# The block sums of two down projections, on VectorE between its low parts instead of on GpSimd in one run

## The chip, the cores and the metric

The kernel runs on one core of a Trainium2 chip. Its engines work side by side, each through its own queue in order: TensorE multiplies matrices, VectorE and ScalarE work element by element, GpSimd does so more slowly, and SyncE issues the DMAs. They wait for each other on semaphores. The metric is the device time of one launch in microseconds (us), the median of three runs.

## What is computed

Two layers of a transformer-like trunk on an input of 1024 tokens by 1024 channels, all in float32. Each layer has a mixer (a gated MLP over chunks in the first, differential attention in the second) and then a convolutional feed-forward part; both stand between RMS norms. The change touches only the last product of the feed-forward part:

```python
def conv_ffn(x, w_up, conv_w, conv_b, w_down):
    h = causal_dwconv(x @ w_up, conv_w, conv_b)
    g, u = h[..., :D_FF], h[..., D_FF:]
    return (jax.nn.gelu(g) * u) @ w_down

# in each of the two layers, after the mixer
y = rmsnorm(h, norm_g[layer, 2])
y = conv_ffn(y, ffn_w_up[layer], ffn_conv_w[layer], ffn_conv_b[layer], ffn_w_down[layer])
h = h + rmsnorm(y, norm_g[layer, 3])
```

Here `x @ w_up` is 1024x1024 by 1024x5632, and the product with `w_down`, the down projection, is 1024x2816 by 2816x1024. It is done twice, once for each layer.

## The kernel before

Float32 matmuls are made of three matmuls in a reduced format. `split` (L167 to L173) takes a tile apart into a high part (a cast on ScalarE, L170) and a low part (the tile minus its high part, on VectorE, L173), and TensorE adds up high x high, high x low and low x high (L162, `PASSES`).

`down` (L459) makes a down projection by a Strassen-Winograd scheme with seven products in place of eight. The activations are cut into four blocks A11, A12, A21, A22 of 512 tokens by 1408 channels, the weights likewise. Sums of weight blocks (T1 to T4) were made earlier, while the feed-forward part ran, and lie in the buffer `td` in HBM. The sums of activation blocks are made here, in place, by `combine` (L482): A21 becomes A21 + A22, then A11 becomes A21 - A11, then A22 becomes A22 - A11 and A12 becomes A12 - A11. The products run in the order A11·B11, A22·T4, A12·B21, A11·T2, A21·T1, A12·B22, A22·T3 (L528 to L552); the first three use blocks as they were loaded, the last four their sums. So a sum may overwrite a block only once its old content has been split, and must be there before the product that uses it.

A block is eleven tiles of 128 channels by 512 tokens, handled in five pairs of two tiles (128x1024 elements) and one piece of one tile (128x512). One block sum is thus five instructions of 128x1024 and one of 128x512, and a down projection has four block sums, 24 instructions, all issued by `nc.gpsimd.tensor_tensor` in L484. `product` (L498) splits activations and weights pair by pair (`operands`, L486) and multiplies: 11 tiles x 4 groups of rows x 3 passes make 132 matmuls of 128x512 for one product. The last two pieces of a product (its tail) are multiplied group by group, so that the four results come out one after another.

How far the splits run ahead of TensorE is set by the buffers: 15 tiles `t8` for activation blocks and their parts, 7 tiles `w4` for the parts of weights, 4 tiles `wr` for weights as they are loaded. A buffer is taken again when its last reader is done. All loads stand in one queue, SyncE's, and a load that waits for a buffer holds up the loads behind it. The order in which instructions stand on each engine is set by a scheduler when the program is built, from the order of the code, the dependences and its own estimate of times; it may move an instruction ahead of others that stand before it in the code.

In the profile the activation tiles are all called t, loaded weights wr, their parts w, matmul results ps.

Of the kernel before, what the change touches and what calls it, by code (L numbers as in the profile page):

```python
# [13 lines left out]
ALU = mybir.AluOpType  # L14
# [46 lines left out]
SHORT_TAIL = 2  # L61
# [3 lines left out]
def trunk(ctx: ExitStack, tc: tile.TileContext, io):  # L65
    nc = tc.nc
# [7 lines left out]
    def nm(s):  # L74
        uid[0] += 1
        return f"{s}_{uid[0]}"

    def t8(dt=F32R, shape=(P, 2, S)):
        return base.tile(list(shape), dt, tag="t8", name=nm("t8"), bufs=15)
# [88 lines left out]
    def split(hi, lo, src, engine=None, pin=False):  # L168

        i = nc.scalar.copy(hi, src)  # L170
        if pin:
            tc.keep_in_program_order(i)
        return (engine or nc.vector).tensor_tensor(lo, src, hi.bitcast(F32), ALU.subtract)  # L173

    def raw_w(src, a, b):
        raw = wpool.tile([P, a, b], F32, tag="wr", name=nm("wr"), bufs=4)
        nc.sync.dma_start(raw, src)
        return raw

    def w4(shape, extra=None):  # L180

        pool, tag, n = extra or (wpool, "w4", 7)
        return pool.tile([P] + list(shape), F32R, tag=tag, name=nm(tag), bufs=n)
# [263 lines left out]
    def weight_blocks(w, o):  # L447
        nk = o.shape[1]
        return {
            "B11": lambda k, n: w[k:k + n, :, 0:512],  # L450
            "B21": lambda k, n: w[nk + k:nk + k + n, :, 0:512],
            "B22": lambda k, n: w[nk + k:nk + k + n, :, 512:1024],
            "T1": lambda k, n: o[0, k:k + n, :, 0],
            "T3": lambda k, n: o[0, k:k + n, :, 1],
            "T4": lambda k, n: o[1, k:k + n, :, 0],
            "T2": lambda k, n: o[1, k:k + n, :, 1],
        }

    def down(l, h_in, h_out, g_post, g_pre, y_next):  # L459

        nk = NFF // 2
        pairs = [(k, min(2, nk - k)) for k in range(0, nk, 2)]
        weights = weight_blocks(io["ffn_down"][l], td[l])
        raw = {}

        def load(a):  # L470
            half, j = int(a[1]) - 1, (int(a[2]) - 1) * nk
            raw[a] = []
            for k in range(0, nk, 4):
                n = min(4, nk - k)
                t = t8(F32, (P, 4, 512))
                nc.sync.dma_start(t[:, :n], pd[l][half, j + k:j + k + n].rearrange("j p c -> p j c"))
                raw[a].append(t)

        def of(a, k, n):
            return raw[a][k // 4][:, k % 4:k % 4 + n]  # L480

        def combine(o, a, b, op):  # L482
            for k, n in pairs:
                nc.gpsimd.tensor_tensor(of(o, k, n), of(a, k, n), of(b, k, n), op)  # L484

        def operands(a, b, k, n, apart=False):  # L486
            x = t8(F32R, (P, 2, 2, 512))
            split(x[:, 0, :n], x[:, 1, :n], of(a, k, n))
            raw = raw_w(weights[b](k, n).rearrange("k p c -> p k c"), n, 512)
            if apart:  # L490
                t = t8(F32R, (P, 2, 2, 512))
                w = t[:, 0, :n], t[:, 1, :n]
            else:
                w = w4((n, 512)), w4((n, 512))
            split(*w, raw)
            return x, w

        def product(a, b, ahead=(), first=None, at=3, tail=SHORT_TAIL, wide=0):  # L498

            out = [bank1() for _ in range(4)]  # L500

            def part(i, k, n, x, w):
                for kt in range(k, k + n):
                    for m, (p, q) in enumerate(PASSES):
                        mm(
                            out[i], x[:, q, kt - k, i * P:(i + 1) * P], w[p][:, kt - k, :],
                            kt == 0 and m == 0, kt == nk - 1 and m == 2,
                        )

            for m, (k, n) in enumerate(pairs[:-tail]):  # L510
                xw = ahead[m] if m < len(ahead) else operands(a, b, k, n)
                for i in range(4):
                    part(i, k, n, *xw)
                if m == at and first:
                    first()
            xws = [operands(a, b, k, n, m >= tail - wide) for m, (k, n) in enumerate(pairs[-tail:])]
            for i in range(4):
                for (k, n), xw in zip(pairs[-tail:], xws):
                    part(i, k, n, *xw)
                yield i, out[i]  # L520

        add = nc.vector.tensor_tensor
        load("A11")
        ahead = [operands("A11", "B11", *pairs[0])]
        yield
        with tc.tile_pool(name=nm("out"), bufs=1) as pool:
            u2, c11, v = (pool.tile([P, 4, 512], F32, tag=n, name=nm(n)) for n in ("u2", "c11", "v"))
            for i, r in product("A11", "B11", ahead, lambda: load("A22")):  # L528
                nc.scalar.copy(u2[:, i], r)
            gp = load_g(pool, g_post)  # L530
            gn = load_g(pool, g_pre) if g_pre is not None else None
            load("A21")
            for i, r in product("A22", "T4", (), lambda: load("A12"), 1):
                nc.scalar.copy(v[:, i], r)

            combine("A21", "A21", "A22", ALU.add)
            combine("A11", "A21", "A11", ALU.subtract)
            combine("A22", "A22", "A11", ALU.subtract)
            for i, r in product("A12", "B21"):
                add(c11[:, i], r, u2[:, i], ALU.add)  # L540
            combine("A12", "A12", "A11", ALU.subtract)
            for i, r in product("A11", "T2"):
                add(u2[:, i], r, u2[:, i], ALU.add)
                nc.gpsimd.tensor_tensor(v[:, i], v[:, i], u2[:, i], ALU.add)
            u4 = t8(F32, (P, 4, 512))
            for i, r in product("A21", "T1"):
                add(u4[:, i], r, u2[:, i], ALU.add)
            for i, r in product("A12", "B22"):
                c12 = pool.tile([P, 512], F32, tag="c12", name=nm("c12"), bufs=2)
                add(c12, r, u4[:, i], ALU.add)  # L550
                end(pool, i, (c11[:, i], c12), h_in, h_out, gp, gn, y_next, n=2)
            for i, r in product("A22", "T3", tail=TAIL, wide=WIDE):  # L552
                add(v[:, i], r, v[:, i], ALU.add)
                add(u4[:, i], r, u4[:, i], ALU.add)
                end(pool, 4 + i, (v[:, i], u4[:, i]), h_in, h_out, gp, gn, y_next, n=2)
# [483 lines left out]
    class Winograd:  # L1039
# [32 lines left out]
        def add(self, o, a, b):  # L1072
            nc.vector.tensor_tensor(o, a, b, ALU.add)  # L1073
# [251 lines left out]
```

## Time and profile before

| | us |
|---|---|
| median of 3 runs | 2198.74 (2196.4 to 2199.98) |
| the profiled execution, its time | 2199.97 |
| its span, first to last instruction | 2198.2 |
| TensorE busy | 2127.0 (97%) |
| VectorE busy | 1696.9 (77%) |
| ScalarE busy | 1095.6 (50%) |
| GpSimd busy | 895.4 (41%) |

The profile is of one execution. Its time is 1.23 us above the median of the runs. The busy share is an average over the whole program: a TensorE that is busy 97% of the time can still lose time in the places where it waits, and where its clock falls after a wait. The two down projections lie from about 747 to 945 us and from about 1967 to 2190 us after the first instruction. A busy VectorE or GpSimd instruction may be a slow one: the profile counts the time from its start to its end, whatever held it up inside.

### The profile page before, as it was taken

What the parts mean: (1) busy time and instruction counts of PE and PEld (TensorE: products, weight loads), DVE (VectorE), ACT (ScalarE), POOL (GpSimd) and SP (SyncE); (2) the same over time, 40 slices, a digit from 0 to 9 for tenths busy, and PEclk for the clock granted to TensorE, in tenths of its full rate; (3) what the DMA queues carried; (4) which work ended last, traced back from release to release, by engine and by line L of the source; (5) the groups of instructions that cost most, each with busy time, mean ns of one, the idle gap of its engine ahead of it and who ended that gap; (6) DMA issues with size and microseconds to landing.
All of it is one profiled execution on the core that took longest, in us unless ns stands there. A gap on an engine that the chain in (4) does not pass through costs nothing.

```text
span 2198.2 us, 27299 instructions
## 1 busy us (share of the span) xinstructions
PE 2127.0 (97%) x10008; PEld 1730.1 (79%) x10008; DVE 1696.9 (77%) x1983; ACT 1095.6 (50%) x1923; POOL 895.4 (41%) x739
## 2 busy tenths in 40 slices
PE   8989998999999999999999999999899999999998
PEld 6868776888888877887777777778688888887786
DVE  5755569888888798688588888866987888878856
ACT  7423445555545544464366665655554555553433
POOL 1463135666666094042001001322565667618512
PEclk9989999999999999999999999999999999999999
DMA  8332422444444652353411110243244444456224
GB/s 316 101 125 77 179 82 98 170 163 157 141 155 161 225 191 92 130 182 105 156 44 44 55 43 20 87 144 116 77 149 140 163 154 153 163 191 230 87 96 167
DMA packets 159270, 292.82 MB, mean 133 GB/s; under 512 B 12704, under 2 KB 77088, under 8 KB 159136
## 3 DMA queue, kind: packets, MB, share of 16 engines
q1 hardware_dynamic: 159136, 291.08, 38.4%
q8 instruction: 78, 1.28, 0.2%
q14 instruction: 56, 0.46, 0.1%
HBM read 214.49 MB, written 76.55 MB: 132 GB/s over the span
## 4 chain that ended last, share of the span: by engine, by line
PE 74%; DVE 9%; ACT 3%; issue 1%; DMA 1%; POOL 0%; DVEq 0%; POOLq 0%; ACTq 0%; SPq 0%
PE ps L162 69%; PE pst L162 2%; DVE t L173 2%; DVE w L173 2%; PE pst L887 1%; ACT e L868 1%; DVE t L1138 1%; PE pst L334 1%; DVE cols L1073 1%; DVE xs L344 0%; DVE e L874 0%; DVE h L381 0%; DMA wr<-td 0%; DVE sm L865 0%; ACT t L1136 0%
## 5 line engine op out<-in xcount | busy, mean ns | idle before, releaser
L162 PE MATMUL ps<-t,w 128*128 128x512 f32 x4848 | 1152.8, 394 | 20.4 <-ACT tm L1069 7.8
L162 PEld LDWEIGHTS ps<-t,w 128*128 128x128 f32 x4848 | 901.1, 189 | 221.6 <-issue 12.3
L162 PE MATMUL ps<-w,t 128*128 128x512 f32 x2512 | 600.5, 396 | 23.6 <-DVE t L173 13.6
L162 PEld LDWEIGHTS ps<-w,t 128*128 128x128 f32 x2512 | 474.7, 191 | 126.4 <-DVE t L173 16.1
L173 DVE TENSOR_TENSOR w<-wr,w 128x512 fp32r<-128x512 f32 (+1 forms) x274 | 333.3, 1224 | 165.1 <-ACT w L170 84.1
L170 ACT CAST w<-wr 128x512 fp32r<-128x512 f32 (+1 forms) x276 | 219.1, 802 | 206.3 <-PE ps L162 196.7
L1138 DVE SCALAR_TENSOR_TENSOR t<-cols,cw,t 128x1023 f32<-128x1023 f32 (+1 forms) x176 | 265.0, 1506 | 18.6 <-ACT t L1136 16.7
L484 POOL TENSOR_TENSOR t<-t,t 128x1024 f32<-128x1024 f32 (+1 forms) x48 | 146.8, 3096 | 116.7 <-PE ps L162 58.4
L173 DVE TENSOR_TENSOR t<-t,t 128x1024 fp32r<-128x1024 f32 (+1 forms) x124 | 179.3, 1477 | 16.6 <-ACT t L170 16.5
L173 DVE TENSOR_TENSOR w<-wt,w 128x512 fp32r<-128x512 f32 x176 | 171.4, 984 | 14.4 <-ACT w L170 14.3
L1069 ACT COPY tm<-ps 128x512 f32<-128x512 f32 x136 | 79.1, 582 | 146.8 <-PE ps L162 146.7
L1027 POOL TENSOR_TENSOR wt<-wr,wr 128x512 f32<-128x512 f32 x44 | 68.0, 1544 | 195.6 <-DMA wr<-in_ffn_up 140.2
L170 ACT CAST t<-t 128x1024 fp32r<-128x1024 f32 (+1 forms) x124 | 105.7, 888 | 74.0 <-PE ps L162 50.4
L1136 ACT ACTIVATE t<-cols,cw 128x1024 f32<-128x1024 f32 x88 | 109.7, 1247 | 60.3 <-DVE cols L1073 60.2
L162 PE MATMUL ps<-t,t 64*128 64x512 f32 (+4 forms) x792 | 129.2, 375 | 0.8 <-ACT e L868 0.4
L376 POOL TENSOR_SCALAR sm<-sm 128x1 f32<-128x1 f32 x32 | 22.3, 698 | 245.6 <-ACT y L374 245.3
L202 POOL TENSOR_SCALAR sm<-sm 128x1 f32<-128x1 f32 (+1 forms) x42 | 12.8, 305 | 264.7 <-ACT ot L907 161.3
L170 ACT CAST w<-wt 128x512 fp32r<-128x512 f32 x176 | 108.0, 622 | 22.7 <-PE ps L162 13.6
L162 PEld LDWEIGHTS ps<-t,t 64*128 64x128 f32 (+1 forms) x792 | 91.1, 187 | 34.5 <-issue 11.2
L868 ACT ACTIVATE e<-ps,sm 128x128 f32<-128x128 f32 (+7 forms) x128 | 94.3, 745 | 28.8 <-DVE sm L860 22.8
L173 POOL TENSOR_TENSOR t<-wr,t 128x1024 fp32r<-128x1024 f32 (+1 forms) x16 | 36.4, 2282 | 168.8 <-ACT t L170 168.8
L1073 DVE TENSOR_TENSOR cols<-ps,tm 128x512 f32<-128x512 f32 x132 | 90.1, 682 | 17.1 <-PE ps L162 15.4
(156 smaller groups left out, 2443.8 us busy)
## 6 DMA issues: line engine op xcount, KB each, us to landing
wr<-in_ffn_up SPq DMA_DIRECT2D x88, 512.0 KB, 4.2
wr<-in_ffn_down SPq DMA_DIRECT2D x94, 256.0 KB, 3.8
pd<-t SPq DMA_DIRECT2D x88, 256.0 KB, 2.6
td<-wr SPq DMA_DIRECT2D x88, 256.0 KB, 2.5
wr<-td SPq DMA_DIRECT2D x40, 512.0 KB, 3.7
t<-pd SPq DMA_DIRECT2D x16, 1024.0 KB, 8.2
wr<-in_ffn_down SPq DMA_DIRECT2D x30, 512.0 KB, 3.6
hd<-h SPq DMA_DIRECT2D x24, 512.0 KB, 2.6
```

The source lines that it names most:

```text
L162: nc.tensor.matmul(o, a, b, start=first, stop=last, skip_group_check=onto)
L170: i = nc.scalar.copy(hi, src)
L173: return (engine or nc.vector).tensor_tensor(lo, src, hi.bitcast(F32), ALU.subtract)
L334: nc.tensor.transpose(pt[:, k * P:(k + 1) * P], xs[:, f:f + P], ident)
L376: nc.gpsimd.tensor_scalar(ss, sq[:, 0:1], sq[:, 1:2], EPS, ALU.add, ALU.add)
L484: nc.gpsimd.tensor_tensor(of(o, k, n), of(a, k, n), of(b, k, n), op)
L868: nc.scalar.activation(e[:, :L], si[i], AF.Exp, bias=negm[:, i:i + 1], accum_out=sm[:, i:i + 1])
L1027: i = nc.gpsimd.tensor_tensor(t1, b12, b11, ALU.subtract)
L1069: nc.scalar.copy(t, o)
L1073: nc.vector.tensor_tensor(o, a, b, ALU.add)
L1136: nc.scalar.activation(tt, src, AF.Identity, bias=c[:, 3:4], scale=c[:, 2:3])
L1138: nc.vector.scalar_tensor_tensor(tt[:, tap:], src[:, :S - tap], c[:, 2 - tap:3 - tap], tt[:, tap:], ALU.mult, ALU.add)
```

## The change

`combine` no longer issues anything. It appends its six instructions to a list, and a new function `some(n)` issues the next n of them, on VectorE. `product` calls `some(2)` after it has split a pair (in the product A22·T4 only from the third pair on, since A21 is being loaded then) and once more at the tail. The calls of `combine` for A21 and A11 move ahead of the product A22·T4, and those for A12 and A22 stand behind A12·B21; calls of `some(len(sums))` issue what is left. The function bodies that are left out here are the same as before.

```diff
@@ -479,9 +479,16 @@
+        sums = []
+
         def combine(o, a, b, op):
+
             for k, n in pairs:
-                nc.gpsimd.tensor_tensor(of(o, k, n), of(a, k, n), of(b, k, n), op)
+                sums.append((of(o, k, n), of(a, k, n), of(b, k, n), op))
+
+        def some(n):
+            for _ in range(min(n, len(sums))):
+                nc.vector.tensor_tensor(*sums.pop(0))
...
             for m, (k, n) in enumerate(pairs[:-tail]):
                 xw = ahead[m] if m < len(ahead) else operands(a, b, k, n)
+                if m > 1 or b != "T4":
+                    some(2)
                 for i in range(4):
                     part(i, k, n, *xw)
...
+            some(4 if tail == SHORT_TAIL else len(sums))
             for i in range(4):
...
             load("A21")
+
+            combine("A21", "A21", "A22", ALU.add)
+            combine("A11", "A21", "A11", ALU.subtract)
             for i, r in product("A22", "T4", (), lambda: load("A12"), 1):
                 nc.scalar.copy(v[:, i], r)
-
-            combine("A21", "A21", "A22", ALU.add)
-            combine("A11", "A21", "A11", ALU.subtract)
-            combine("A22", "A22", "A11", ALU.subtract)
             for i, r in product("A12", "B21"):
                 add(c11[:, i], r, u2[:, i], ALU.add)
+            some(len(sums))
             combine("A12", "A12", "A11", ALU.subtract)
+            combine("A22", "A22", "A11", ALU.subtract)
             for i, r in product("A11", "T2"):
                 add(u2[:, i], r, u2[:, i], ALU.add)
                 nc.gpsimd.tensor_tensor(v[:, i], v[:, i], u2[:, i], ALU.add)
+            some(6 - (12 - len(sums)))
...
             for i, r in product("A21", "T1"):
                 add(u4[:, i], r, u2[:, i], ALU.add)
+            some(len(sums))
```

The scheduler decides where the sums then stand. VectorE's queue in the first down projection, before the change, at the splits of the second product A22·T4. L173 are low parts; a row names the result, the two inputs and the shape. t_975, t_979, t_986, t_990 are low parts of pairs 0 to 3 of A22, w_978, w_982, w_989, w_993 those of T4's pairs 0 to 3:

```order
L173 TENSOR_TENSOR w_978_6236<-wr_6233,w_977_6235 128x1024
L173 TENSOR_TENSOR t_975_6230<-t_955_6152,t_975_6230 128x1024
L173 TENSOR_TENSOR t_979_6263<-t_955_6152,t_979_6263 128x1024
L173 TENSOR_TENSOR w_982_6269<-wr_6266,w_981_6268 128x1024
L173 TENSOR_TENSOR t_986_6302<-t_956_6154,t_986_6302 128x1024
L173 TENSOR_TENSOR t_990_6335<-t_956_6154,t_990_6335 128x1024
L173 TENSOR_TENSOR w_989_6308<-wr_6305,w_988_6307 128x1024
L173 TENSOR_TENSOR w_993_6341<-wr_6338,w_992_6340 128x1024
```

Nothing else stands between the low parts. After the change, the same place of VectorE's queue up to the low part of T4's pair 1 (L491 are the sums; t_968 to t_970 hold A21, t_955 to t_957 A22, t_923 to t_925 A11, four tiles or three in each):

```order
L173 TENSOR_TENSOR w_978_6236<-wr_6233,w_977_6235 128x1024
L491 TENSOR_TENSOR t_968_6220<-t_968_6220,t_955_6152 128x1024 x2
L173 TENSOR_TENSOR t_975_6230<-t_955_6152,t_975_6230 128x1024
L491 TENSOR_TENSOR t_969_6222<-t_969_6222,t_956_6154 128x1024
L173 TENSOR_TENSOR t_979_6263<-t_955_6152,t_979_6263 128x1024
L491 TENSOR_TENSOR t_969_6222<-t_969_6222,t_956_6154 128x1024
L173 TENSOR_TENSOR w_982_6269<-wr_6266,w_981_6268 128x1024
```

Four sums now stand among the first low parts, two of them ahead of the first low part of A22. The rows that follow these after the change, up to T4's pair 3:

```order
L491 TENSOR_TENSOR t_970_6224<-t_970_6224,t_957_6156 128x1024
L491 TENSOR_TENSOR t_970_6224<-t_970_6224,t_957_6156 128x512
L491 TENSOR_TENSOR t_923_5922<-t_968_6220,t_923_5922 128x1024 x2
L173 TENSOR_TENSOR t_986_6302<-t_956_6154,t_986_6302 128x1024
L491 TENSOR_TENSOR t_924_5924<-t_969_6222,t_924_5924 128x1024
L173 TENSOR_TENSOR t_990_6337<-t_956_6154,t_990_6337 128x1024
L491 TENSOR_TENSOR t_924_5924<-t_969_6222,t_924_5924 128x1024
L491 TENSOR_TENSOR t_925_5926<-t_970_6224,t_925_5926 128x1024
L173 TENSOR_TENSOR w_989_6308<-wr_6305,w_988_6307 128x1024
L173 TENSOR_TENSOR w_993_6343<-wr_6340,w_992_6342 128x1024
```

Seven more sums stand ahead of the low part w_989. From the first sum to w_989 the queue has 16 instructions of 128x1024 and one of 128x512, of which the last is w_989 itself. In the second down projection VectorE's queue has as many, 16 and one, from its first sum to the low part of T4's pair 2; there one sum, not two, stands ahead of T4's pair 0. The remaining sums follow in both among the splits of A22·T4's tail and behind them, and the last seven, A22's last piece and A12's six, between the splits of A12·B21, so that all are queued ahead of the adding up of A12·B21's results.

TensorE's queue changes at one place, the start of pair 2 of A22·T4 in the first down projection. Before (ps_971 and ps_972 are the results of the first two groups of rows, w_988 and w_989 the high and low part of the weights):

```order
L162 MATMUL ps_971_6226<-w_988_6307,t_986_6302 128x512 x2
L162 MATMUL ps_971_6226<-w_989_6308,t_986_6302 128x512
L162 MATMUL ps_971_6226<-w_988_6307,t_986_6302 128x512 x2
L162 MATMUL ps_971_6226<-w_989_6308,t_986_6302 128x512
L162 MATMUL ps_972_6227<-w_988_6307,t_986_6302 128x512 x2
```

and after:

```order
L162 MATMUL ps_971_6226<-w_988_6307,t_986_6302 128x512 x2
L162 MATMUL ps_972_6227<-w_988_6307,t_986_6302 128x512 x2
L162 MATMUL ps_971_6226<-w_989_6308,t_986_6302 128x512
L162 MATMUL ps_971_6226<-w_988_6307,t_986_6302 128x512 x2
L162 MATMUL ps_971_6226<-w_989_6308,t_986_6302 128x512
```

The first matmul that needs the low part w_989 stands two matmuls later. GpSimd's queue loses its 48 sums; ScalarE's queue is the same, and SyncE's differs in two loads that change places.

## Rows read from the trace of the kernel before

**Rows 1.** The page's first part: busy us (share) x instructions of each engine.

```profile
PE 2127.0 (97%) x10008; PEld 1730.1 (79%) x10008; DVE 1696.9 (77%) x1983; ACT 1095.6 (50%) x1923; POOL 895.4 (41%) x739
```

**Rows 2.** Chain that ended last, first down projection: start us, us, what.

```profile
775.86 7.63 DMA wr<-td
...
784.60 3.34 DVE w L173
...
799.65 2.78 DVE t L173
...
836.46 2.75 DVE t L173
```

**Rows 3.** Timeline of TensorE, first down: start, us, instructions, [idle before <-releaser].

```profile
746.93 40.51 PE L162 MATMUL ps<-w,t 128*128 128x512 f32 x178
787.99 12.33 PE L162 MATMUL ps<-w,t 128*128 128x512 f32 x53 [0.55 <-DVE w L173]
802.48 30.48 PE L162 MATMUL ps<-w,t 128*128 128x512 f32 x126 [2.16 <-DVE t L173]
833.72 1.66 PE L162 MATMUL ps<-w,t 128*128 128x512 f32 x6 [0.76 <-DVE t L173]
839.26 104.43 PE L162 MATMUL ps<-w,t 128*128 128x512 f32 x449 [3.88 <-DVE t L173]
943.53 6.28 PE L162 MATMUL ps<-t,t 128*128 128x512 f32 x27
```

**Rows 4.** Timeline of TensorE, second down projection.

```profile
1967.51 40.51 PE L162 MATMUL ps<-w,t 128*128 128x512 f32 x178
2009.72 12.35 PE L162 MATMUL ps<-w,t 128*128 128x512 f32 x53 [1.71 <-DVE w L173]
2024.19 30.46 PE L162 MATMUL ps<-w,t 128*128 128x512 f32 x126 [2.12 <-DVE t L173]
2055.42 1.65 PE L162 MATMUL ps<-w,t 128*128 128x512 f32 x6 [0.76 <-DVE t L173]
2060.96 104.54 PE L162 MATMUL ps<-w,t 128*128 128x512 f32 x449 [3.88 <-DVE t L173]
2165.33 24.64 PE L162 MATMUL ps<-t,t 128*128 128x512 f32 x108
```

**Rows 5.** Stretches: us, busy us (x) PE, PEld, DVE, ACT, POOL; PEclk, DMA share, GB/s.

```profile
770.00:844.00 74.00, 66.65 (x273) 53.55 (x273) 69.34 (x25) 26.79 (x32) 73.58 (x24) 0.93 0.47 161
1989.00:2063.00 74.00, 65.52 (x274) 52.69 (x274) 70.55 (x26) 28.14 (x34) 73.09 (x24) 0.95 0.48 167
```

**Rows 6.** Timeline of GpSimd: the sums of both down projections.

```profile
770.06 73.58 POOL L484 TENSOR_TENSOR t<-t,t 128x1024 f32<-128x1024 f32 x24 [58.37 <-PE ps L162]
...
1989.29 71.07 POOL L484 TENSOR_TENSOR t<-t,t 128x1024 f32<-128x1024 f32 x23 [57.68 <-DMA t<-pd]
```

**Rows 7.** Timeline of VectorE, first down: as the sums begin and after their end.

```profile
767.81 1.22 DVE L173 TENSOR_TENSOR w<-wr,w 128x1024 fp32r<-128x1024 f32 x1 [4.80 <-PE ps L162]
770.02 1.23 DVE L173 TENSOR_TENSOR t<-t,t 128x1024 fp32r<-128x1024 f32 x1 [0.98 <-ACT t L170]
771.59 2.99 DVE L173 TENSOR_TENSOR t<-t,t 128x1024 fp32r<-128x1024 f32 x1 [0.34 <-ACT t L170]
...
853.41 1.22 DVE L173 TENSOR_TENSOR w<-wr,w 128x1024 fp32r<-128x1024 f32 x1
854.55 1.22 DVE L173 TENSOR_TENSOR t<-t,t 128x1024 fp32r<-128x1024 f32 x1
...
932.10 0.68 DVE L173 TENSOR_TENSOR t<-t,t 128x512 fp32r<-128x512 f32 x1
932.70 0.68 DVE L550 TENSOR_TENSOR c<-ps,t 128x512 f32<-128x512 f32 x1
```

**Rows 8.** A float32 tensor_tensor on VectorE, L1143: ns min/median/max, first and last start.

```profile
L1143 DVE TENSOR_TENSOR t<-t,t x44: 1210/1218/2325, 362.3 to 1973.7; 128x1024 f32<-128x1024 f32 x44
```

**Rows 9.** ScalarE's cast of T4's pair 2, first down: what it waited for.

```profile
783.51 1.05 ACT L170 CAST w<-wr 128x1024 fp32r<-128x1024 f32 x1 [0.88 <-DMA wr<-td]
```

## The prediction

> **What bounds the kernel now.** First the page's busy times: TensorE is busy 97% [rows 1], so time is lost only where it waits or is slowed. Then the chain of waits in the first down projection: it leaves TensorE in three places, all between 775 and 839 us, and each time comes back to it through low parts on VectorE [rows 2]. TensorE's timeline gives the waits: 0.55, 2.16, 0.76 and 3.88 us, 7.35 together, each ended by a low part [rows 3]. In the second down projection there are four again, 8.47 together [rows 4].
>
> What the two projections lose in all is read from the same rows. From 746.93 to 943.53 us, 196.60 us, TensorE has 178 + 53 + 126 + 6 + 449 = 812 matmuls [rows 3]. The first 178 run without a wait at 40.51 / 178 = 0.2276 us each, so 812 would take 184.8 us: 11.8 us are lost. From 1967.51 to 2165.33, 197.82 us, as many matmuls lose 13.0 us [rows 4]. Together **24.8 us**. Not all of it is waiting: in the 74 us around the sums the granted clock is 0.93 and 0.95 [rows 5], so part of the time ran at 1.2 in place of 2.4 GHz, which costs 74 x (0.07 + 0.05) = 8.9 us. The clock fell after TensorE had waited, so this part goes if the waits go.
>
> Why the low parts are late: GpSimd's sums run from 770.06 to 843.6 and from 1989.29 on [rows 6], and in just that time VectorE's low parts are slow. One of 128x1024 takes 1.22 us at 767.81 and at 853.41, but 2.99 at 771.59 [rows 7] and 3.34 at 784.60 [rows 2]. VectorE is busy 69.34 and 70.55 of the 74 us with 25 and 26 instructions [rows 5], so its low parts come at the rate at which it can make them, and TensorE overtakes it.
>
> **The change part by part.** *The sums leave GpSimd.* They had the 73.58 us beside the low parts [rows 6]; GpSimd's other work there is none. A low part should go back to its own price: back to back, starts are 854.55 - 853.41 = 1.14 us apart for 128x1024 and 932.70 - 932.10 = 0.60 for 128x512 [rows 7].
>
> *The sums join VectorE.* A float32 tensor_tensor of the same shape and kinds as a sum takes 1.218 us in the median [rows 8], as long as a low part alone, so a sum is taken at 1.14 and 0.60 too: 20 x 1.14 + 4 x 0.60 = 25.2 us for each projection. With 25 low parts at 1.14 or less (28.5) VectorE then has at most 53.7 us of work in a stretch that lasts some 62 us once nothing is lost (74 - 11.8), so it no longer is the slowest there. The bounds of a sum's price: 1.14 from the rows of the same shape, and 1.22 plus a little if each waits for the end of the one before.
>
> *What is queued behind the sums.* VectorE works in order, so what matters is the low parts behind sums. The first sum of each projection needs A21 to be loaded; GpSimd's first sum began at 770.06 and 1989.29 [rows 6], so VectorE's is taken to begin then (in the second, its low part at 1988.4 moves behind this sum, which costs nothing while TensorE is still in the product before). The critical one is the low part of T4's pair 2: 16 instructions of 128x1024 and one of 128x512 from the first sum to its end make 16 x 1.14 + 0.60 = 18.8 us. It is done at 788.9 and 2008.1. Its weights are no limit: their cast started at 783.51 [rows 9], behind loads that the change doesn't touch. TensorE came to this low part at 787.99 - 0.55 = 787.4 and at 2009.72 - 1.71 = 2008.0 [rows 3, 4]; in the first projection its queue now has two other matmuls before it, 2 x 0.23, which makes it 787.9. So it will wait 788.9 - 787.9 = 1.0 and 0.1 us, where it waited 0.55 and 1.71. The low parts before it have more room: pair 0's, behind two sums, is done some 3.4 us after the first sum, 773.5, and the product begins at 787.4 less 50 matmuls, 776.0.
>
> *After that* the queue empties faster than TensorE asks. Behind w_989 follow, up to the last low part of A22·T4's tail, four instructions of 128x1024 (one of them a sum) and three of 128x512 (one a sum): 4 x 1.14 + 3 x 0.60 = 6.4 us, so 795.3; before, TensorE stood still for it from 800.3 on [rows 3]. The second projection has six and three there, 8.6 us, 2016.7 against a need at about 2020. Among A12·B21's splits stand the last seven sums: ten low parts and five sums of 128x1024, two and two of 128x512, 19.5 us in the 30 us of a product. The waits of 2.16, 0.76 and 3.88 us should go, and the fallen clock with them: after the wait of 1.71 us at 2009.72 the next 53 matmuls still took 12.35 / 53 = 0.233 us each [rows 4], so a wait of 1.0 us is taken to leave the clock alone.
>
> *The rest* has no cost on the path. The two loads that change places on SyncE, and GpSimd's queue, which only gets shorter, wait for nothing that is late. From 839 us on TensorE ran 449 matmuls without a wait [rows 3], with sums of A22 and A12 long done; these products find the same order of VectorE's queue as before.
>
> **The sum.** 24.8 lost - 1.1 for the new waits = 23.7 us. From the profiled execution's own 2199.97 us this gives 2176.3; the median of the runs is 1.23 lower, so 2175.0 against 2198.74.
>
> **The rivals.** *Sums that come out slower (A).* If VectorE's instructions don't overlap at all, each is 0.1 us longer, 16 of them 1.6: the waits at pair 2 become 2.6 and 1.7 us. Waits of about 2.16 us were the ones behind which the clock fell; the first such stretch has 126 matmuls in 30.48 us [rows 3], 1.8 us over 126 x 0.2276. With one such fall in each projection 2.6 + 1.7 + 2 x 1.8 = 7.9 of the 24.8 stay lost, 16.9 are gained: 2182. For it: eleven of the sums do stand ahead of that one low part. Against it: starts 1.14 apart in [rows 7].
>
> *A wait that comes back at A11·T2 (B).* The largest wait before, 3.88 us, came there. If the sums of A12 and A22 between A12·B21's splits keep VectorE behind, it stays, with 0.76 ahead of it and the fallen clock behind it, 104.43 - 449 x 0.2276 = 2.2 us: 2 x 6.8 = 13.7 of the 24.8, and 1.1 at pair 2. Gained are 10.0: 2189. Against it: 19.5 us of work in 30.
>
> *VectorE becomes the bound (C), the slower side.* If the low parts are slow for a reason of their own, not for GpSimd's sums, VectorE keeps its 69.34 and 70.55 us [rows 5] and gets 25.2 on top: 94.5 and 95.8 in a stretch of 74, so TensorE waits 20.5 and 21.8 us more: 2198.7 + 42 = 2241. It decides from the point where a low part beside no GpSimd work still takes more than about 1.9 us ((74 - 25.2) / 25). For it, a little: the low part that began at 770.02, with the first sum, still took 1.23 us. Against it: all before that and from the last sum's end on are fast too [rows 6, 7]. The Trainium skill has a rule by which this rival would be the forecast: its page Perfetto Trace Analysis, section Identifying the Most-Contended Engine, says to read for VectorE and GpSimd the engine with the highest occupancy as the bottleneck, and 94% busy is VectorE's here; by that rule, adding work to it makes the kernel slower, about 2241 as just worked out. The trace speaks against taking the occupancy at its word, since most of a busy time of 2.99 us is not work.
>
> **How the numbers follow.** The forecast has 0.72, A 0.13, B 0.06, C 0.05; 0.04 are left for gains that vanish elsewhere, so that the time stays within 0.2%, about what a measurement of this kernel can tell from no change. Faster are the forecast, A and B: 0.91. Slower is C: 0.05. Same: 0.04. The range goes from all 24.8 us gained and a median 2.5 lower, as the runs spread, 2171.5, to beyond A, 2186; it leaves out B, C and the rest.
>
> **What would show it.** In the changed kernel's profile no sum is on GpSimd; low parts and sums of 128x1024 on VectorE take 1.22 us in both down projections; TensorE has one wait of about 1 us at the third pair of A22·T4 of the first projection and nearly none else in them; the granted clock there is 1.00; and 812 matmuls take 186 us from the start of A11·B11. Low parts over 2 us would make C right, a wait of 3 us at A11·T2 B, a fallen clock after pair 2 A. Waits of TensorE outside the two projections that are not in the kernel before would make the sum wrong.

## The result and the profile after

The changed kernel takes **2173.69 us** in the median (2172.96 to 2175.61), the kernel before, on the same chip, 2197.57: a ratio of 0.9892, with a 95% interval of 0.988 to 0.9904. The prediction was 2175.0, in a range of 2171.5 to 2186.

The profiled execution took 2173.85 us, its span is 2172.0. Busy times first, as in [rows 1]:

```profile
PE 2115.5 (97%) x10008; PEld 1722.7 (79%) x10008; DVE 1662.3 (77%) x2031; ACT 1094.9 (50%) x1923; POOL 748.5 (34%) x691
```

VectorE has 48 instructions more, the sums, and yet is busy 34.6 us less than in [rows 1]. So its sums were paid for by shorter low parts. Both are seen in the trace. All sums by their line (ns min/median/max, first and last start), and VectorE's timeline in the first down projection (start, us, instruction, [idle before <-releaser]), which answers to [rows 7]:

```profile
L491 DVE TENSOR_TENSOR t<-t,t x48: 677/1214/1227, 771.7 to 2032.0; 128x1024 f32<-128x1024 f32 x40, 128x512 f32<-128x512 f32 x8
```

```profile
769.09 1.23 DVE L173 TENSOR_TENSOR w<-wr,w 128x1024 fp32r<-128x1024 f32 x1 [4.80 <-PE ps L162]
771.72 2.36 DVE L491 TENSOR_TENSOR t<-t,t 128x1024 f32<-128x1024 f32 x2 [1.40 <-DMA t<-pd]
774.00 1.22 DVE L173 TENSOR_TENSOR t<-t,t 128x1024 fp32r<-128x1024 f32 x1
775.14 1.21 DVE L491 TENSOR_TENSOR t<-t,t 128x1024 f32<-128x1024 f32 x1
...
787.09 2.35 DVE L491 TENSOR_TENSOR t<-t,t 128x1024 f32<-128x1024 f32 x2
789.36 2.35 DVE L173 TENSOR_TENSOR w<-wr,w 128x1024 fp32r<-128x1024 f32 x2
```

No sum takes over 1.227 us, and the low parts between them take 1.22, where [rows 7] had 2.99. Starts are 1.14 us apart: 774.00, 775.14.

What TensorE makes of it, in the first and then the second down projection, against [rows 3, 4]:

```profile
748.21 40.96 PE L162 MATMUL ps<-w,t 128*128 128x512 f32 x180
790.63 143.55 PE L162 MATMUL ps<-w,t 128*128 128x512 f32 x632 [1.46 <-DVE w L173]
934.02 6.29 PE L162 MATMUL ps<-t,t 128*128 128x512 f32 x27
...
1955.12 184.22 PE L162 MATMUL ps<-w,t 128*128 128x512 f32 x812
2139.17 24.64 PE L162 MATMUL ps<-t,t 128*128 128x512 f32 x108
```

Of four waits in each projection one is left in all, 1.46 us. The 812 matmuls take 185.81 us in place of 196.60, and 184.05 (1955.12 to 2139.17) in place of 197.82: 10.79 and 13.77 us less, **24.56** together. The stretches of the first projection (us, busy us (x) of PE, PEld, DVE, ACT, POOL; PEclk, DMA share, GB/s) answer to [rows 5]:

```profile
746.90:931.50 184.60, 183.14 (x808) 151.38 (x807) 131.26 (x130) 86.12 (x106) 11.73 (x11) 1.00 0.48 165
770.00:832.00 62.00, 60.54 (x267) 49.83 (x266) 51.69 (x50) 27.20 (x34) 0.00 (x0) 1.00 0.58 202
```

The granted clock is 1.00 where it was 0.93, and around the sums VectorE does 50 instructions in 51.69 us where it did 25 in 69.34.

The spans differ by 2198.2 - 2172.0 = 26.2 us. The two projections give 24.56. The first begins 1.28 us later than before, the time between them is 2.88 us shorter (1021.10 from 934.02 to 1955.12; it was 1023.98), and the end is 0.04 us shorter. Between the projections the code is the same; in the executions of the experiments below this time is 1019.8 (without sums) to 1024.7 us (sums fixed in place). So the 2.88 us are taken as scatter from one execution to the next.

### The profile page after: what moved, and what is told of

Read it like the earlier page. It is cut to its first block, busy times and chain, and to the rows that moved or that the text cites. A ratio compares the mean times of both kernels' runs of the same rounds, so it can differ in the third digit from the quotient of the medians.

```text
span 2172.0 us, 27266 instructions
## 1 busy us (share of the span) xinstructions
PE 2115.5 (97%) x10008; PEld 1722.7 (79%) x10008; DVE 1662.3 (77%) x2031; ACT 1094.9 (50%) x1923; POOL 748.5 (34%) x691
## 3 DMA queue, kind: packets, MB, share of 16 engines
q8 instruction: 78, 1.28, 0.2%
## 4 chain that ended last, share of the span: by engine, by line
PE 69%; DVE 9%; ACT 4%; DMA 3%; issue 2%; POOL 2%; SPq 0%; DVEq 0%; POOLq 0%; ACTq 0%
PE ps L162 65%; PE pst L162 2%; DVE t L173 2%; DVE w L173 1%; DVE t L1151 1%; ACT e L881 1%; PE pst L900 1%; PE pst L334 1%; DMA wr<-in_ffn_up 1%; DVE cols L1086 1%; DMA t<-pd 1%; DVE e L887 0%; DVE xs L344 0%; DMA td<-wr 0%; DVE sm L878 0%
## 5 line engine op out<-in xcount | busy, mean ns | idle before, releaser
L162 PE MATMUL ps<-w,t 128*128 128x512 f32 x2512 | 590.2, 392 | 10.5 <-ACT w L170 6.1
L162 PEld LDWEIGHTS ps<-w,t 128*128 128x128 f32 x2512 | 469.4, 188 | 108.3 <-ACT w L170 6.3
L173 DVE TENSOR_TENSOR w<-wr,w 128x512 fp32r<-128x512 f32 (+1 forms) x274 | 292.1, 1072 | 168.7 <-ACT w L170 77.5
L173 DVE TENSOR_TENSOR w<-wt,w 128x512 fp32r<-128x512 f32 x176 | 171.4, 984 | 16.4 <-ACT w L170 16.2
L173 DVE TENSOR_TENSOR t<-t,t 128x1024 fp32r<-128x1024 f32 (+1 forms) x124 | 133.9, 1108 | 14.4 <-ACT t L170 14.0
L555 POOL TENSOR_TENSOR v<-v,u 128x512 f32<-128x512 f32 x8 | 12.0, 1498 | 306.8 <-DVE u L554 306.8
L173 POOL TENSOR_TENSOR t<-wr,t 128x1024 fp32r<-128x1024 f32 (+1 forms) x16 | 36.4, 2286 | 166.3 <-ACT t L170 158.1
```

Of the source, the lines that this page charges most:

```text
L162: nc.tensor.matmul(o, a, b, start=first, stop=last, skip_group_check=onto)
```

## The experiments

All ratios are against the kernel before, run on the same chip. "Wait" is TensorE's in the first down projection, and "low part" the duration of one of 128x1024 there up to 860 us (behind that GpSimd adds up v, and a low part beside these additions takes up to 2.32 us even where GpSimd has no sums).

| kernel | median us | ratio (95%) | wait us | low part us |
|---|---|---|---|---|
| changed kernel | 2173.69 | 0.9892 (0.988 to 0.9904) | 1.46 | 1.22 |
| sums on VectorE in one run | 2176.05 | 0.9897 (0.9877 to 0.9918) | 1.28 | 1.22 |
| sums on VectorE, fixed in place | 2173.78 | 0.9894 (0.9879 to 0.9909) | 0 | 1.22 |
| sums on GpSimd in pieces | 2197.15 | 1.0002 (0.9993 to 1.0011) | 7.36 | to 3.42 |
| no sums | 2171.86 | 0.9885 (0.987 to 0.99) | 0 | 1.22 |
| no sums, GpSimd memsets | 2171.99 | 0.9879 (0.9858 to 0.9901) | 0 | 1.22 |
| no sums, GpSimd with one input | 2173.79 | 0.9888 (0.9866 to 0.9909) | 0 | to 1.63 |
| no sums, GpSimd with two inputs, 128x512 | 2185.5 | 0.9941 (0.9919 to 0.9962) | 4.12 | to 2.32 |
| half of the sums on GpSimd | 2173.84 | 0.9889 (0.9872 to 0.9907) | 1.29 | to 3.42 |
| the other half on GpSimd | 2214.22 | 1.0073 (1.0056 to 1.0089) | 15.28 | to 3.42 |
| no sums, GpSimd 128x1024 early | 2184.2 | 0.9935 (0.9915 to 0.9955) | 3.30 | to 3.43 |
| the same, later | 2193.12 | 0.9979 (0.9967 to 0.9991) | 6.71 | to 3.43 |
| sums three times on VectorE | 2244.39 | 1.0211 (1.0192 to 1.0229) | 26.5 | 1.22 |

**Which part of the change counts: the engine or the pieces?** The kernel before with one word changed, and the changed kernel with its pieces on GpSimd:

```diff
-                nc.gpsimd.tensor_tensor(of(o, k, n), of(a, k, n), of(b, k, n), op)
+                nc.vector.tensor_tensor(of(o, k, n), of(a, k, n), of(b, k, n), op)
```

> The kernel before with one word changed: the block sums are issued on VectorE, in one run as they stood in the code, not in pieces. Theory (the gain comes from GpSimd no longer working beside VectorE; the scheduler spreads the sums by itself): VectorE's queue at A22·T4 comes out the same as in the changed kernel up to the names, so the time does too, 2174 us, ratio 0.989 to 0.990. Rival (the pieces in the code make the gain): 24 sums at 1.14 us stand in a block ahead of low parts, TensorE waits some 15 us or more in each projection, time 2190 or more.

```diff
-                nc.vector.tensor_tensor(*sums.pop(0))
+                nc.gpsimd.tensor_tensor(*sums.pop(0))
```

> The changed kernel with its sums in pieces, but issued on GpSimd. Theory: low parts of 128x1024 beside the sums take some 3 us again, TensorE waits four times in each projection and its clock falls; time 2194 to 2200, ratio 0.998 to 1.002. Rival (what counts is when the sums are made and in which pieces): 2180 or less.

The engine is all of it: 0.9897 with one word, 1.0002 with the pieces alone. TensorE's longest waits with the pieces on GpSimd are the old ones of [rows 3]:

```profile
805.13 30.47 PE L162 MATMUL ps<-w,t 128*128 128x512 f32 x126 [2.14 <-DVE t L173]
836.37 1.66 PE L162 MATMUL ps<-w,t 128*128 128x512 f32 x6 [0.77 <-DVE t L173]
841.90 104.49 PE L162 MATMUL ps<-w,t 128*128 128x512 f32 x449 [3.87 <-DVE t L173]
```

"In pieces" is no part of the gain, since the scheduler interleaves sums that the code writes in one run: around the splits of A22·T4 in the first projection VectorE runs the same order in the one-word kernel and in the changed one. To see pieces that are where the code puts them, the sums were fixed against the scheduler:

```diff
-                nc.vector.tensor_tensor(*sums.pop(0))
+                tc.keep_in_program_order(nc.vector.tensor_tensor(*sums.pop(0)))
```

> The changed kernel with each sum kept at its place in the code, so that none stands ahead of the low part w_989 of T4's third pair. Theory: the wait of 1.46 us there goes or shrinks to that of the weights' landing (cast done at 786.3, low part at 787.5, so under 0.2 us); no other wait appears as long as A11·T2's first low part, now behind one sum of A12 and one result's adding up, is done some 2 us before it is needed; time 1 to 1.5 us under the changed kernel, 2172.5, which these rounds can hardly tell from it. Rival (a wait comes back at A11·T2 since sums now run into that product): 2 to 4 us in each projection and a fallen clock, 2178 to 2184.

The first sum now stands behind T4's pair 2, at 785.34 us, and the last wait is gone:

```profile
745.68 184.22 PE L162 MATMUL ps<-w,t 128*128 128x512 f32 x812
```

1.46 us are 0.07% of the time, less than these runs can tell: the ratio is the same.

**What do the sums cost on VectorE?** The sums were left out; the last four products then use the blocks as loaded:

```diff
-                nc.vector.tensor_tensor(*sums.pop(0))
+                sums.pop(0)
```

> The changed kernel without the block sums: the last four products multiply the blocks as they were loaded. This is the floor of what moving the sums can bring. Theory (VectorE has room for the sums): only the wait at the third pair of A22·T4 in the first projection goes, 1.5 us, so 2172 us, ratio 0.988 to 0.989. Rival (the sums on VectorE still cost several us somewhere): 2165 or less.

2171.86 us is the floor, and the changed kernel stands within 1.8 us of it: 50 us of sums on VectorE cost next to nothing. By the ratios the change brings 1.08% and leaving the sums out 1.15%, with intervals that overlap.

**Is it reading that collides?** On this floor GpSimd got work on data that nobody uses, at the place of the sums: 44 additions of two inputs, 96 memsets, or 64 multiplications of one input by a constant, all of 128x512:

```diff
+            scratch = pool.tile([P, 512], F32, tag="c12", name=nm("scratch"), bufs=2)
+            for _ in range(44):
+                nc.gpsimd.tensor_tensor(scratch, u2[:, 0], u2[:, 1], ALU.add)
             load("A21")
```

> No block sums (the last four products multiply the blocks as loaded); in their place GpSimd makes 44 sums of 128x512 of two parts of u2 into a tile that nobody reads, from the end of A11·B11 on, so no low part depends on GpSimd. Theory (two engines that read SBUF at once hold each other up): low parts of 128x1024 take 2 to 3.4 us while these run, TensorE waits in A22·T4 and A12·B21 as in the kernel before; 2190 to 2200 us. Rival (low parts waited for the sums' data or buffers): low parts 1.22 us, 2172.

> The same, but after one such sum GpSimd does 96 memsets of 128x512 in place of the 43 others: it is busy and writes, but reads nothing. Theory in its narrow form (it is GpSimd's reading that collides with a VectorE instruction of two inputs): low parts 1.22 us, 2172. Theory in its wide form (any GpSimd access to SBUF collides): low parts 1.5 us or more, TensorE waits, 2178 to 2195.

> The same with 64 tensor_scalar instructions of 128x512 on GpSimd, which read one input and write one output. Narrow form of the theory: low parts are slowed, by less for each GpSimd instruction than in the run with two inputs: 1.5 to 2.5 us, time between 2175 and 2195. If only two-input instructions collide: low parts 1.22, 2172.

Two low parts back to back on VectorE, beside the additions, beside the multiplications and beside the memsets (one alone there):

```profile
813.36 4.54 DVE L173 TENSOR_TENSOR w<-wr,w 128x1024 fp32r<-128x1024 f32 x2
```

```profile
807.21 3.07 DVE L173 TENSOR_TENSOR t<-t,t 128x1024 fp32r<-128x1024 f32 x2
```

```profile
806.71 1.23 DVE L173 TENSOR_TENSOR w<-wr,w 128x1024 fp32r<-128x1024 f32 x1 [4.93 <-PE ps L162]
```

So memsets cost nothing (GpSimd was busy with them for 55.97 us), one input some 0.3 us for each low part, two inputs about 1.1 for each. The Trainium skill, page SBUF — State Buffer, section Who interferes with whom, says that a VectorE instruction with two inputs in SBUF contends with a GpSimd instruction that reads SBUF and not with one that only writes it. The three rows agree with that. What each would cost the kernel was expected too high: the multiplications 2175 to 2195 (2173.79), the additions 2190 to 2200 (2185.5). A low part that is slowed is thus not yet time lost.

Beside the same additions stand two other VectorE instructions, the adding up of a result (c, of whose inputs one is a matmul result ps) and a multiplication of two tiles (y):

```profile
833.77 0.68 DVE L552 TENSOR_TENSOR c<-ps,u 128x512 f32<-128x512 f32 x1
835.24 1.68 DVE L375 TENSOR_TENSOR y<-c,gb 128x512 f32<-128x512 f32 x1 [0.79 <-ACT y L374]
```

Without sums they take 0.68 and 0.69 us (830.74 and 832.21 us there). So the one that reads a matmul result is not slowed, and the one with both inputs in tiles is.

**How much of it can be hidden?** Of the kernel before, the sums of two blocks were put on VectorE, the others left on GpSimd:

```diff
-                nc.gpsimd.tensor_tensor(of(o, k, n), of(a, k, n), of(b, k, n), op)
+                (nc.vector if o in ("A21", "A11") else nc.gpsimd).tensor_tensor(of(o, k, n), of(a, k, n), of(b, k, n), op)
```

> The kernel before with the sums of A21 and A11 on VectorE and those of A22 and A12 left on GpSimd: each engine has half. Theory (the two hold each other up, the sums on VectorE too): from about 784 us on all VectorE instructions of 128x1024 take some 3 us; w_989, behind some five of them, is done about 10 us late, and the tail of A22·T4 later still; each projection loses 8 to 20 us, time 2185 to 2212, no better than the middle between the two kernels. Rival (the work is shared, so each engine has less to do): 2174 or less.

The expectation fell: 2173.84 us, as with all sums on VectorE. And yet the collision is there. Low parts alone from 796 to 836 us (us, VectorE busy, GpSimd busy at this line, PEclk, DMA share, GB/s), without sums and with half of them on GpSimd:

```profile
796.00:836.00 40.00, 16.24 (x15) 0.00 (x0) 1.00 0.33 107
```

```profile
796.00:836.00 40.00, 35.88 (x16) 0.00 (x0) 1.00 0.36 113
```

Some 18 us more in slowed low parts (35.88 - 16.24, less one instruction more), and TensorE did not wait there. Two ways to explain this were set against each other, that the place counts (low parts come close together up to 796 us and further apart behind that) and that the dose counts. The same 12 additions of 128x1024, ahead of 24 memsets and behind them, with the sums left out (after one addition of 128x512, which holds both back until the data is there); the lines shown have the memsets first:

```diff
+            scratch = pool.tile([P, 2, 512], mybir.dt.bfloat16, tag="c12", name=nm("scratch"), bufs=2)
+            nc.gpsimd.tensor_tensor(scratch[:, 0], u2[:, 0], u2[:, 1], ALU.add)
+            for _ in range(24):
+                nc.gpsimd.memset(scratch, 0.0)
+            for _ in range(12):
+                nc.gpsimd.tensor_tensor(scratch, u2[:, 0:2], u2[:, 2:4], ALU.add)
             load("A21")
```

> Leaves out the sums, so the last four products use the unsummed blocks and the output is not the reference's. In their place GpSimd, on data that nobody uses, runs ahead of A22.T4 first 12 additions of two inputs of 128x1024 and then 24 memsets. The run with half of the sums on GpSimd showed all low parts at some 3.4 us from 796 to 836 us with TensorE not waiting; before 796 no sum of GpSimd ran there. Theory (the place decides: between 769 and 796 us the low parts come close together, 12 of them in 27 us, later 14 to 16 in 40 us): the additions run from about 775 to 815 us, the low parts pair up with them at some 3.4 us, some three low parts are missing by 796 us, and TensorE waits near 803 us for about 2 us as with all sums on GpSimd (2.1 us), no longer after 815; with a fall of the clock that goes with such a wait (1 to 3 us) a projection loses 2 to 5 us: 2175 to 2182 us, against 2171.9 without sums. Rival (the dose decides, 40 us of collision are taken up wherever they lie): no wait, 2171 to 2174 us, as its twin with the additions later.

> As its twin (sums left out, the output is not the reference's; GpSimd works on data that nobody uses), with the same 12 additions of two inputs and 24 memsets, but the memsets ahead: the additions begin 14 to 28 us later, at 790 to 803 us, and end at 825 to 840 us, in the stretch where the low parts come far apart. Theory (the place decides): low parts of about 3.4 us there, TensorE doesn't wait, 2171 to 2174 us. Rival (the dose decides): the same time as its twin, whatever that is.

With the additions early the wait came where it was expected, up to 804.09 us, but it was 3.30 us long, not 2, and 2184.2 us lies above the range. Of the additions later both expectations were missed: later is worse, 2193.12 against 2184.2. TensorE and VectorE with the additions later, from 797.12 to 835.27 us:

```profile
823.68 5.73 PE L162 MATMUL ps<-w,t 128*128 128x512 f32 x24 [1.16 <-DVE t L173]
830.35 1.66 PE L162 MATMUL ps<-w,t 128*128 128x512 f32 x6 [0.94 <-DVE t L173]
835.88 103.61 PE L162 MATMUL ps<-w,t 128*128 128x512 f32 x449 [3.87 <-DVE t L173]
```

```profile
797.81 3.27 DVE L173 TENSOR_TENSOR t<-t,t 128x1024 fp32r<-128x1024 f32 x1
803.98 2.93 DVE L173 TENSOR_TENSOR w<-wr,w 128x1024 fp32r<-128x1024 f32 x1 [2.90 <-PE ps L162]
806.83 6.78 DVE L173 TENSOR_TENSOR t<-t,t 128x1024 fp32r<-128x1024 f32 x2
...
833.00 2.82 DVE L173 TENSOR_TENSOR t<-t,t 128x512 fp32r<-128x512 f32 x1
```

From these rows a third reading came. A product's 132 matmuls take TensorE 132 x 184.22 / 812 = 29.9 us. Its 12 low parts take VectorE 10 x 1.14 + 2 x 0.60 = 12.6 us back to back, which leaves **17.3 us spare**. By this reading slowed low parts cost time only where what they take beyond their own 1.22 and 0.69 us exceeds this. Summed over the 12 low parts of A12·B21 in the first projection, run by run, beside TensorE's waits for them:

| kernel | beyond their own time, us | less 17.3 | waits, us |
|---|---|---|---|
| no sums | 0.1 | none | 0 |
| GpSimd 128x1024 early | 7.6 | none | 0 |
| GpSimd with two inputs, 128x512 | 12.6 | none | 0 |
| half of the sums on GpSimd | 16.6 | none | 0 |
| sums on GpSimd in pieces | 21.7 | 4.4 | 0.77 + 3.87 = 4.64 |
| kernel before | 21.7 | 4.4 | 0.76 + 3.88 = 4.64 |
| GpSimd 128x1024 later | 23.5 | 6.2 | 6.71 |

The half stays just below since GpSimd has to wait there: the sums of A12 overwrite what the low parts of A12·B21 read, and while GpSimd stands still some low parts take 1.21 us:

```profile
822.62 3.32 POOL L484 TENSOR_TENSOR t<-t,t 128x1024 f32<-128x1024 f32 x1 [2.30 <-DVE t L173]
827.10 2.78 POOL L484 TENSOR_TENSOR t<-t,t 128x1024 f32<-128x1024 f32 x1 [1.16 <-DVE t L173]
```

In the second projection the half is at 17.9 us, 0.6 above the spare, and TensorE doesn't wait there either.

The early additions cost their wait in A22·T4, 3.30 us at 13.4 us beyond, so that product has less spare; its weights and blocks are still being loaded then. In the second projection they cost 3.26 us there and 0.84 early in A12·B21, where the low parts take only 8.8 us beyond their own time; perhaps since that product started with less ahead of it. The waits beside the 128x512 additions, 4.12 us, come after 842 us, in A11·T2, where the low parts take only 8.1 us beyond their own time. There the adding up of results (c) and multiplications (y) stand on VectorE too; but six such instructions at 0.60 us leave 13.7 us spare by the same count. So the sum over a product does not explain these waits. Even without sums the first low parts of A11·T2 come back to back, from 837.50 us on, and such a crowd may have nothing to spare where the product in the mean has; no run shows which.

This reading was made to fit these runs. It says something that had not been tried: sums on VectorE cost nothing because 25.2 us fit into the spare time of three products, and three times as many must not fit. To each of the fixed sums two more VectorE instructions in place were added, which take the larger of a block and itself:

```diff
-                tc.keep_in_program_order(nc.vector.tensor_tensor(*sums.pop(0)))
+                o, a, b, op = sums.pop(0)
+                for a, b, op in ((a, b, op), (o, o, ALU.max), (o, o, ALU.max)):
+                    tc.keep_in_program_order(nc.vector.tensor_tensor(o, a, b, op))
```

> The changed kernel with the sums fixed where the code puts them, and each sum followed on VectorE by two more additions of its kind in place (the larger of a block and itself, which leaves the block as it is): 72 instead of 24 per projection. Theory (a product leaves VectorE a spare, and that decides for sums and collisions alike): a product of 132 matmuls takes TensorE 29.9 us (evictions of two neighbouring products start at 831.56 and 861.46 us), its 12 low parts take VectorE 12.6 us back to back (ten at 1.14, two at 0.60), so 17.3 us are spare per product, 52 over the three products in which the sums stand. The 24 sums of the changed kernel take 25.2 of these. 72 take 75.6 and with 5 us of evictions VectorE is some 29 us behind over three products, less what low parts made ahead give back: TensorE waits 15 to 30 us per projection, 2204 to 2240 us with falls of the clock. Rival (VectorE's queue holds TensorE up only where GpSimd slows it, its own additions always fall into idle time): 2172 to 2178 us.

TensorE waits 26.5 us in the first projection and 27.8 in the second, within the 15 to 30 expected; the two longest waits of the first:

```profile
827.25 44.06 PE L162 MATMUL ps<-w,t 128*128 128x512 f32 x180 [10.07 <-DVE t L173]
...
901.09 2.08 PE L162 MATMUL ps<-w,t 128*128 128x512 f32 x4 [10.61 <-DVE t L173]
```

The time, 2244.39, is 4 us above the range. From 747.29 to 967.67 us the projection lasts 220.4 us, 36.3 over the 184.05 without a wait; 26.5 are waits, and the other 9.8 are matmuls at the lower clock (0.93 in the mean from 747 to 968 us), which the range had too low. VectorE stands idle for only 4.1 us from the first of these instructions, at 786.63 us, to the last, at 907.83, so it is the bound there. Where a wait falls is set by the order: the low part that ends the one of 10.07 us stands behind 16 such instructions in a row, from 809.40 us on.

**The other half.** The sums of A21 and A11 on GpSimd, those of A22 and A12 on VectorE:

```diff
-                nc.gpsimd.tensor_tensor(of(o, k, n), of(a, k, n), of(b, k, n), op)
+                (nc.gpsimd if o in ("A21", "A11") else nc.vector).tensor_tensor(of(o, k, n), of(a, k, n), of(b, k, n), op)
```

> The other half: the sums of A21 and A11 on GpSimd, those of A22 and A12 on VectorE, where the order built puts the first of them behind the third low part of A22.T4. It takes what GpSimd's seventh sum writes. GpSimd's sums run from 773 us, at 2.3 us apart when VectorE stands still and 3.4 us when not, so the seventh ends at 789 to 797 us; until then VectorE, which takes its queue in order, stands still with the low parts of A22.T4 behind it. Theory (the place and the order of the queue decide, not the count of sums on GpSimd): TensorE waits some 5 to 15 us per projection in A22.T4, with a fall of the clock: 2183 to 2205 us. Rival (what counts is how many sums GpSimd makes, as the run with the other 12 on it cost nothing): 2172 to 2177 us.

Slower than the kernel before, and above the range. It is another mechanism: VectorE's queue stands still for 7.01 us behind its first sum of A22, which waits for GpSimd, with low parts behind it; from then on it has sums and slowed low parts to do in turn. VectorE's and TensorE's rows:

```profile
781.91 3.40 DVE L484 TENSOR_TENSOR t<-t,t 128x1024 f32<-128x1024 f32 x1 [7.01 <-POOL t L484]
```

```profile
795.23 8.37 PE L162 MATMUL ps<-w,t 128*128 128x512 f32 x24 [6.07 <-DVE w L173]
809.59 146.32 PE L162 MATMUL ps<-w,t 128*128 128x512 f32 x634 [5.99 <-DVE w L173]
```

The sum that VectorE waited for was GpSimd's third, done at 781.88, and not the seventh as expected, which was done at 794.09; and still the waits are 15.28 us; the projection lasts from 750.59 to 955.75 us, 21.1 over 184.05. As many sums on GpSimd as in the run that cost nothing, and 40 us between the two.

## Why the prediction was right, point by point

- **What was lost before, 24.8 us in the two projections, as waits and fallen clock.** 24.56 us came back there, where the sum had 23.7. Two terms were off, and against each other. Without a wait a projection takes 184.05 us, 0.2267 for each of 812 matmuls and not the 0.2276 taken from the first 178, so 12.55 + 13.77 = 26.3 us were lost, 1.5 more than 24.8; and the new wait keeps 185.81 - 184.05 = 1.76 us, not 1.1. That the runs gained 23.9 us in the median is thus closer to the forecast than its terms were, in part by luck. The other 1.64 us by which the spans differ (2.88 + 0.04 - 1.28) lie outside the projections. The part put down to the clock went with the waits: it is granted at 1.00 through the first projection and at 1.00 from 1955 to 2139 us.
- **GpSimd's sums slow the low parts.** Shown by both one-part runs: with the engine alone changed the low parts take 1.22 us and the gain is there, with the pieces alone neither.
- **A sum on VectorE at 1.14 us.** The sums start 1.14 us apart. That they cost so little was argued from 53.7 us of work in 62; measured are 51.69 us.
- **The wait at pair 2, 1.0 us in the first and 0.1 in the second projection.** Measured: 1.46 and none. The mis-sized term is the moment of the first sum. It was taken to begin where GpSimd's did; moved with the product that is 770.06 + 1.28 = 771.34, and A21 landed such that it began at 771.72. The 18.8 us from there held: w_989 begins at 789.36, and the next low part 1.14 us later, at 790.50. In the second projection the first sum began 20.98 us after A11·B11's first matmul, not 21.78.
- **No wait after that.** 632 matmuls run without one, through A12·B21 and A11·T2.
- **Rival A (slower sums)** has 1.22 us and starts 1.14 apart against it; its price was a little high, 16 x (1.22 - 1.14) = 1.3 us and not 1.6. **Rival B** read the wait of 3.88 us at the wrong place: it did not come at A11·T2 but among the last matmuls of A12·B21. It ended at 839.26 us, with that product's last low part, and the product's results are added up only behind that (the two rows below). By the reading above the slowed low parts of A12·B21 itself made it, 21.7 us beyond their own time. It is gone with them, and no wait came at A11·T2 in its place.
- **Rival C (VectorE the bound)** was rightly given little, but the prediction's reason for it was only half of the matter. It held VectorE's 94% busy for mostly stalled time, which the runs bear out; the triple sums show that VectorE does become the bound once its real work passes the spare 17 us of a product. The rule of the Trainium skill that was named there, page Perfetto Trace Analysis, section Identifying the Most-Contended Engine, reads the bottleneck off the highest occupancy. The prediction took that to be VectorE's, but in both stretches GpSimd's is higher, 73.58 and 73.09 of 74 us against 69.34 and 70.55 [rows 5]: the rule names GpSimd there, and taking work off GpSimd is what helped. VectorE's own occupancy said little of its work: 50 us of added work made it less busy, and 100 more made the kernel slower than before.

VectorE in the kernel before, on rival B:

```profile
836.38 2.82 DVE L173 TENSOR_TENSOR t<-t,t 128x512 fp32r<-128x512 f32 x1
...
844.65 0.68 DVE L540 TENSOR_TENSOR c<-ps,u 128x512 f32<-128x512 f32 x1
```

What the expectations for half of the sums, for the additions of 128x512, for the multiplications and for the later additions had wrong is one thing: they took no account, or none by product, of what VectorE has spare. Slowed low parts cost time beyond that in A12·B21; the waits of 4.12 us beside the additions of 128x512, in A11·T2, do not follow from it.

Open: how much A22·T4 and A11·T2 have to spare was not measured by itself. That half of the sums cost nothing because GpSimd waits for VectorE is argued from rows; no run changed that wait alone.

## What to carry to other kernels

If instructions of VectorE take two or three times their usual duration in some stretch, look at what GpSimd does there before you count VectorE as full: moving GpSimd's work onto VectorE can make both the work and the stretch shorter. Whether it fits is estimated for each product (or loop step) as TensorE's time less VectorE's instructions at their undisturbed spacing, and so is whether a collision hurts at all; where instructions come in a crowd, the estimate is too kind. Of a half-way split the order of the in-order queue has to be looked up first: the same dozen sums on GpSimd cost nothing or 40 us, depending on whether VectorE's own instructions wait for them.

## What the runs showed of the hardware that was not expected

- The strength of the collision goes with GpSimd's inputs and size: a low part of 128x1024 took 1.23 us beside memsets, up to 1.63 beside operations with one input, 2.3 beside two-input additions of 128x512 and 3.4 beside such of 128x1024.
- GpSimd is slowed as well: its additions of 128x512 took 86.23 / 44 = 1.96 us beside low parts; in the run with memsets the first one took 1.29 us (at 774.28). Its sums of 128x1024 follow each other some 3.35 us apart in the kernel before, and 2.35 apart in the run with the other half while VectorE stood still (starts at 777.11, 779.46 and 781.82 us). As 2.35 + 1.14 = 3.49 is little more than 3.35, the two may be taking turns; that is an estimate from these numbers, and no run tests it.

```profile
774.60 86.23 POOL L544 TENSOR_TENSOR scratch<-u 128x512 f32<-128x512 f32 x44 [61.57 <-ACT u L539]
```
